# The opening of a two-layer trunk kernel: w_up's first five output tiles fed by feature slices, modulation tile by tile at first, its weights laid out as whole tiles

## The chip, the cores and the metric

The kernel runs on one core of a Trainium2 chip. The metric is the device time of one execution in microseconds, as the median of several runs. A core has a matrix engine (PE), a vector engine (DVE), a scalar engine (ACT), GpSimd (POOL) and a sync engine (SP, which here only issues transfers), and 16 DMA engines that move data between HBM and the on-chip buffer. Each engine has its own list of instructions; semaphores order them against each other. A matmul reads its operands from the on-chip buffer and adds into a PSUM bank.

## The reference, cut to what matters

The whole computation is a two-layer trunk (an mLSTM layer, an attention layer, each followed by a gated feed-forward net) over 256 latent and 256 context tokens of width 1024. The change lies in its first few steps:

```python
def _modulation(cond, w, b):
    m = jax.nn.silu(cond) @ w + b
    return jnp.split(m[:, None, :], 6, axis=-1)

def _modulate(x, shift, scale):
    return x * (1 + scale) + shift
...
        ml = _modulation(c, ada_w[i], ada_b[i])
        mc = _modulation(c_ctx[None, :], ada_w[i], ada_b[i])
        hl = _modulate(x, ml[0], ml[1])
        hc = _modulate(xc, mc[0], mc[1])
...
    x_m = h @ w_up
```

So before the first large product `h @ w_up` (512 tokens x 1024 features by 1024 x 2048) can begin, the shift and the scale of layer 0 (two of the six parts of a 1024 x 6144 product with the two condition vectors) must be known, at least for the features that the product reads first.

## The kernel before

Everything is kept transposed: features on the 128 partitions, the 512 tokens along the row. A product in full precision is made of three matmuls (`mm3`): each operand is split into a rounded part "hi" (made by ACT, a CAST) and the rest "lo" (made by DVE, a subtraction that needs the cast), and hi x hi, hi x lo, lo x hi are added. A split of a tile is therefore always an ACT instruction and then a DVE instruction.

**start_up** does the following, for feature tiles k = 0..7 (128 features each) and the first `NUP` = 5 output tiles m of w_up:

- loads, issued by SP in the order of the table LOADS: `a` loads modulation weights (256 features of shift and scale at a time, GROUPS, eight transfers of 256 KB into four buffers of 512 KB), `x` two feature tiles of tokens (256 KB each), `r` one output tile's weights of w_up, all eight feature tiles of it (512 KB);
- compute, in the order of the table STEPS, which fixes the order on PE, DVE and ACT: `S` splits a buffer of modulation weights, `A` multiplies it with the condition vectors (result `adar`), `C` copies the sums, `T` transposes them on PE (`adat`), `O` adds the bias and writes shift and scale of that group (`mod0`), `E` modulates one token tile (half on DVE, half on ACT), `H` splits it (`hT`), `W` splits half of an output tile's weights, `V` with k and m is one `mm3` of feature tile k into output tile m, `D` some dummy matmuls on zeros. 40 `V` steps make 120 matmuls of 128 x 512.

Group 0 (features 0 to 255) must be whole before any `E`, and with it any `V`, can run. After start_up, `w_up` goes through the other eleven output tiles, 24 matmuls each.

**The weight stream.** From then on all weights come through a class Stream: `_load` issues a 512 KB load into a `raw` buffer (three of them at this stage), `_split` makes hi and lo of it in one of `NB` = 3 buffers with the tag `w`, `use` hands them out. Loads and splits run ahead as far as buffers are free: a split needs a free `w` buffer, a load a free `raw` buffer. In start_up the same three `w` buffers hold the split weights of output tiles 0, 1 and 2, and three `raw` buffers their loads.

**What sets the order.** Only the instructions inside start_up's `manual_schedule` block keep the order of STEPS among themselves. All others, the stream's loads and splits among them, are put into each engine's list by a scheduler that reckons with its own times, and they can come to stand between the steps. Once built, each engine's list is fixed. SP's loads take eight semaphores (DMAHW0 to DMAHW7) in turn, and a load waits for the one that used its semaphore before.

Of the kernel before, what the change touches and what calls it, by code (L numbers as in the profile page):

```python
# [7 lines left out]
F32 = mybir.dt.float32  # L8
F32R = mybir.dt.float32r
# [5 lines left out]
D = 1024  # L15
SEQ = 256
CTX = 256
T = SEQ + CTX
DEPTH = 2
GRID_W = 64  # L20
EPS = 1e-6
# [3 lines left out]
H0 = 4  # L25
H1 = 8
# [3 lines left out]
CW = 1024  # L30

NB, NRAW, NU, NS = 3, 3, 31, 15
# [18 lines left out]
STEPS = (  # L51
# [3 lines left out]
    "W41 V53 C3 T3 O3 V43 E6 V44 V54 V34 H6 V60 V61 V62 E7 H7 V70 V71 V72 V63 V73 V74 V64").split()  # L55

# [17 lines left out]
def _plan():  # L74
# [6 lines left out]

    for m in range(16):
        add(("up", m, 0), 1024)
# [52 lines left out]
def _pack(i):  # L136
    ids, _ = _plan()
    ws = np.zeros((len(ids), 128, CW), np.float32)
# [57 lines left out]
    parts = {  # L196
        "cond": np.stack([col(i["c"][0]), col(i["c_ctx"])], -1).reshape(128, 16),
        "ln_g": col(i["ln_g"]), "ln_b": col(i["ln_b"]),
        "mcw": col(i["m_conv_w"][0]), "mcb": col(i["m_conv_b"][0]),
        "fcw0": col(i["ffn_conv_w"][0]), "fcb0": col(i["ffn_conv_b"][0]),  # L200
        "fcw1": col(i["ffn_conv_w"][1]), "fcb1": col(i["ffn_conv_b"][1]),
        "ada_b": col(i["ada_b"][0, :2 * D]),
        "ada_c": col(i["ada_b"]),
# [4 lines left out]
    for k, v in parts.items():  # L208
# [13 lines left out]
    rope = np.stack([np.tile(cc, (1, H1)), np.tile(ss, (1, H1))], 0).astype(np.float32)  # L222

    tok = np.concatenate([i["ctx"][0], i["x"][0]], 0)
    tokT = np.ascontiguousarray(tok.T.reshape(8, 128, T))
    arrays = {
        "ws": ws, "sm": np.ascontiguousarray(sm), "rope": np.ascontiguousarray(rope),
        "tok": np.ascontiguousarray(tok), "tokT": tokT,
        "ada_w": np.ascontiguousarray(i["ada_w"]),
        "adaT": np.ascontiguousarray(i["ada_w"].transpose(0, 2, 1)).reshape(2, 6, 8, 128, D),  # L230
# [7 lines left out]
class Stream:  # L238
# [20 lines left out]
    def ring(self, j):  # L259
        return [x for x in self.bufs if x[0] <= j][-1]  # L260

    def skip(self, n):
        self.nl = self.ns = self.nu = n

# [93 lines left out]
class K:  # L358
# [36 lines left out]
    def smc(self, name):  # L395
        o, n = self.off[name]
        return self.sm[:, o:o + n]

# [24 lines left out]
    def setup(self):  # L423
        nc, p = self.nc, self.pool
        a = self.a
        self.sm = p.tile([128, a["sm"].shape[1]], F32, name="sm")
        nc.sync.dma_start(self.sm, a["sm"])
        b1 = self.smc("ada_b")[:, 8:16]
# [33 lines left out]

    def ada_mm(self, pr, i, parts):

        for x in parts:
            for kk in range(2):
                k = 2 * i + kk
                self.nc.tensor.matmul(pr[0:4], self.condr[:, k, :], x[:, kk * 512:(kk + 1) * 512],
                                      start=k == 0 and x is parts[0], stop=k == 7 and x is parts[1])

    def ada_copy(self, pr):
        r = self.s2("adarow")
        self.nc.scalar.copy(r[0:4], pr[0:4])
        return r
# [93 lines left out]

    def h_split(self, k):
        h = self.u("hT")  # L570
        self.split(h[:, 0, :], h[:, 1, :], self.xT[k])
        self.hT.append(h)

    def start_up(self):

        nc, st = self.nc, self.st
        self.hT = []
        self.xcd = self.dr.tile([16, 128, 512], F32, name="xcd")
        self.xmd = self.dr.tile([16, 128, 512], F32, name="xmd")
        self.t2d = {(n, p, j): self.dr.tile([128, 1024], F32, name="t2d")  # L580
                    for n, a, b in (("v", 2, 4), ("y", 1, 6)) for p in range(a) for j in range(b)}
        self.xA, self.x1, self.xc, self.xcr = {}, {}, [], []
        w, ps, raws = [], [], []
        src = self.a["ada_w"][0]
        self.adaw, self.xT = {}, []
        for op, g in LOADS:
            f0, f1 = GROUPS[g] if op != "r" else (0, 0)
            if op == "a":
                wd = 128 * (f1 - f0)
                nk = 512 // wd  # L590
                self.adaw[g] = []
                for k in range(8):
                    if k % nk == 0:
                        t = self.uf("adaw")
                        self.adaw[g].append(t)
                    ap = bass.AP(tensor=src.tensor, offset=src.offset + k * 128 * 6 * D + f0 * 128,
                                 ap=[[6 * D, 128], [D, 2], [1, wd]])
                    c = k % nk * 2 * wd
                    nc.sync.dma_start(t[:, c:c + 2 * wd].rearrange("p (a b) -> p a b", a=2), ap)
            elif op == "x":  # L600
                for i in range(f0, f1):
                    x = self.s2("xT")
                    nc.sync.dma_start(x, self.a["tokT"][i])
                    self.xT.append(x)
            else:
                n, _ = st.ids["up", g, 0]
                r = self.pool.tile([128, 1024], F32, tag="raw" if g < 3 else "ar", name="raw0",
                                   bufs=NRAW if g < 3 else 2)
                nc.sync.dma_start(r, st.ws[n])
                raws.append(r)  # L610

        w3 = [self.pool.tile([128, 2, CW], F32R, tag="w", name="w", bufs=NB) for _ in range(3)]

        def wsplit(m, i):
            if i == 0:
                if m < 3:
                    h, l = w3[m][:, 0], w3[m][:, 1]
                elif m == 3:
                    h, l = [self.pool.tile([128, CW], F32R, tag="acc", name="w0", bufs=2) for _ in range(2)]
                else:  # L620
                    h, l = [self.pool.tile([128, CW], F32R, tag="u", name="w0", bufs=NU) for _ in range(2)]
                w.append((h, l))
                ps.append(self.ps("up"))
            c = slice(i * 512, (i + 1) * 512)
            self.split(w[m][0][:, c], w[m][1][:, c], raws[m][:, c])

        e = mybir.EngineType
        idle = self.ps("idle")
        rows, parts, made = {}, {}, [0] * NUP
        with self.tc.manual_schedule(engines={e.PE, e.DVE, e.Activation}):  # L630
            for step in STEPS:
                op, n = step[0], [int(x) for x in step[1:]]
                g = n[0]
                if op == "S":
                    parts[g, n[1]] = self.ada_split(self.adaw[g][n[1]])
                elif op == "A":
                    if n[1] == 0:
                        rows[g] = self.ps("adar")
                    self.ada_mm(rows[g], n[1], parts.pop((g, n[1])))
                elif op == "C":  # L640
                    rows[g] = self.ada_copy(rows[g])
                elif op == "T":
                    rows[g] = self.ada_T(g, rows[g])
                elif op == "O":
                    self.ada_cols(g, rows.pop(g))
                elif op == "E":
                    self.mod_tile(g)
                elif op == "H":
                    self.h_split(g)
                elif op == "W":  # L650
                    wsplit(g, n[1])
                elif op == "V":
                    k, m = n
                    c = slice(k * 128, (k + 1) * 128)
# [3 lines left out]
                else:  # L658
                    for _ in range(g):
                        nc.tensor.matmul(idle, self.zero[:, 0:128], self.zero, start=True, stop=True)  # L660
        for m in range(NUP):
            self.up_evac(m, ps[m])
# [1123 lines left out]
def build(tc, off, a, out):  # L1786
    es = ExitStack()
    with es:
# [4 lines left out]
        k.setup()  # L1793
        st.skip(NUP)
        k.start_up()
# [175 lines left out]
```

## Time and profile before

| what | value |
|---|---|
| median of 3 runs | 1377.26 us (1376.98 to 6290.27) |
| the profiled execution's own time | 1378.52 us |
| its span in the profile | 1376.7 us |
| PE, DVE, ACT busy | 98%, 78%, 52% of the span |
| clock granted to PE, mean | 0.997 |

One of the three runs took 6290.27 us; the other two lie within 0.3 us of each other. The span is the stretch from the first to the last instruction. A row of the timeline reads: start in us, length in us, engine, line of the kernel, operation, output <- input, shapes, how many were merged into the row, and in brackets how long the engine was idle before it and what ended the wait. A table by windows gives for each stretch the busy time of each engine, the share of the DMA engines' time that was used, and the GB/s they moved. PE's matmuls overlap, so their lengths add up to more than the time they take; the distance from start to start is what one costs.

### The profile page before, as it was taken

What the parts mean: (1) busy time and instruction counts of PE and PEld (TensorE: products, weight loads), DVE (VectorE), ACT (ScalarE), POOL (GpSimd) and SP (SyncE); (2) the same over time, 40 slices, a digit from 0 to 9 for tenths busy, and PEclk for the clock granted to TensorE, in tenths of its full rate; (3) what the DMA queues carried; (4) which work ended last, traced back from release to release, by engine and by line L of the source; (5) the groups of instructions that cost most, each with busy time, mean ns of one, the idle gap of its engine ahead of it and who ended that gap; (6) DMA issues with size and microseconds to landing.
All of it is one profiled execution on the core that took longest, in us unless ns stands there. A gap on an engine that the chain in (4) does not pass through costs nothing.

```text
span 1376.7 us, 18622 instructions
## 1 busy us (share of the span) xinstructions
PE 1350.6 (98%) x6581; PEld 1122.9 (82%) x6581; DVE 1075.7 (78%) x1748; ACT 720.9 (52%) x1242; POOL 121.1 (9%) x215
## 2 busy tenths in 40 slices
PE   7999999999999999999999999999999999999997
PEld 3788888888788888878898888888878898888886
DVE  7698756677598696878789978767888889788873
ACT  6675444445544555374643343334556667466660
POOL 0122000011011011120001000000001001000100
PEclk9999999999999999999999999999999999999999
DMA  9789848789666374756747877646897436355760
GB/s 332 240 305 322 283 159 245 240 283 301 218 199 202 104 231 133 250 197 219 243 142 241 300 238 229 223 143 209 297 270 236 140 100 211 103 186 188 253 200 31
DMA packets 97900, 297.58 MB, mean 216 GB/s; under 512 B 12136, under 2 KB 24808, under 8 KB 97808
## 3 DMA queue, kind: packets, MB, share of 16 engines
q1 hardware_dynamic: 68672, 218.52, 48.4%
q0 software_dynamic: 17472, 57.57, 13.3%
q10 hardware_dynamic: 11664, 20.32, 4.0%
q8 instruction: 51, 0.84, 0.2%
q14 instruction: 41, 0.34, 0.1%
HBM read 262.90 MB, written 33.46 MB: 215 GB/s over the span
## 4 chain that ended last, share of the span: by engine, by line
PE 88%; DVE 5%; DMA 4%; ACT 2%; issue 1%; SPq 0%; ACTq 0%; DVEq 0%
PE fin L1313 8%; PE fin L387 6%; PE fin L388 6%; PE fin L389 6%; PE tok L387 6%; PE tok L389 6%; PE tok L388 6%; PE y L388 4%; PE y L389 4%; PE y L387 4%; PE qk L387 4%; PE qk L389 4%; PE qk L388 4%; PE up L388 2%; PE up L387 2%; PE up L389 2%
## 5 line engine op out<-in xcount | busy, mean ns | idle before, releaser
L329 DVE TENSOR_TENSOR w<-raw,w 128x1024 fp32r<-128x1024 f32 (+3 forms) x290 | 347.7, 1202 | 149.5 <-ACT w L326 147.3
L326 ACT CAST w<-raw 128x1024 fp32r<-128x1024 f32 (+3 forms) x290 | 300.1, 1037 | 289.7 <-PE fin L389 78.6
L508 DVE SCALAR_TENSOR_TENSOR junk<-ar,bc 128x1024 f32<-128x1024 f32 x128 | 155.7, 1216 | 4.5 <-ACT bc L550 2.2
L388 PE MATMUL fin<-h,w 128*128 128x512 f32 (+1 forms) x376 | 141.2, 376 | 0.0
L389 PE MATMUL fin<-h,w 128*128 128x512 f32 (+1 forms) x376 | 140.9, 376 | 0.0
L387 PE MATMUL fin<-h,w 128*128 128x512 f32 (+1 forms) x376 | 140.8, 376 | 0.1
L1313 PE MATMUL fin<-h,w 128*128 128x256 f32 (+1 forms) x640 | 112.9, 339 | 0.0
L1313 PEld LDWEIGHTS fin<-h,w 128*128 128x128 f32 x640 | 98.1, 189 | 14.7
L387 PE MATMUL qk<-xc,w 128*128 128x512 f32 x256 | 100.7, 393 | 0.0
L389 PE MATMUL qk<-xc,w 128*128 128x512 f32 x256 | 99.9, 390 | 0.0
L388 PE MATMUL qk<-xc,w 128*128 128x512 f32 x256 | 99.9, 390 | 0.0
L388 PEld LDWEIGHTS fin<-h,w 128*128 128x128 f32 x376 | 70.8, 188 | 13.0 <-DVE h L1205 0.2
L387 PEld LDWEIGHTS fin<-h,w 128*128 128x128 f32 x376 | 70.6, 188 | 13.2 <-ACT h L1204 0.3
L389 PEld LDWEIGHTS fin<-h,w 128*128 128x128 f32 x376 | 70.8, 188 | 12.7
L387 PEld LDWEIGHTS qk<-xc,w 128*128 128x128 f32 x256 | 48.1, 188 | 10.0 <-issue 0.4
L389 PEld LDWEIGHTS qk<-xc,w 128*128 128x128 f32 x256 | 48.1, 188 | 10.0
L388 PEld LDWEIGHTS qk<-xc,w 128*128 128x128 f32 x256 | 48.1, 188 | 9.6
L387 PE MATMUL up<-hT,w 128*128 128x512 f32 x128 | 50.3, 393 | 0.2 <-ACT hT L392 0.2
L388 PE MATMUL up<-hT,w 128*128 128x512 f32 x128 | 50.1, 391 | 0.3 <-DVE hT L393 0.3
L389 PE MATMUL up<-hT,w 128*128 128x512 f32 x128 | 49.9, 390 | 0.0
L389 PE MATMUL tok<-w,hT 128*128 128x512 f32 x128 | 49.8, 389 | 0.0
L387 PE MATMUL tok<-w,hT 128*128 128x512 f32 x128 | 49.8, 389 | 0.0
(455 smaller groups left out, 3152.5 us busy)
## 6 DMA issues: line engine op xcount, KB each, us to landing
raw<-in_ws SPq DMA_DIRECT2D x287, 512.0 KB, 4.4
ar<-in_adaT SPq DMA_DIRECT2D x80, 512.0 KB, 4.6
adaw<-in_ada_w SPq DMA_DIRECT2D x32, 256.0 KB, 6.5
t2d<-raw ACTq DMA_DIRECT2D x13, 512.0 KB, 6.5
raw<-t2d SPq DMA_DIRECT2D x13, 512.0 KB, 4.8
raw<-in_ws POOLq DMA_DIRECT2D x13, 512.0 KB, 7.5
zr<-fd ACTq DMA_DIRECT2D x33, 128.0 KB, 4.3
xmd<-xr POOLq DMA_DIRECT2D x16, 256.0 KB, 4.9
```

The costliest lines, as they stand in the source:

```text
L326: k.nc.scalar.copy(h[:, :cols], src)
L329: k.nc.vector.tensor_sub(l[:, :cols], src, h[:, :cols])
L387: mm(out, w[0], x[0], start=start, stop=False, skip_group_check=on)
L388: mm(out, w[0], x[1], start=False, stop=False, skip_group_check=on)
L389: mm(out, w[1], x[0], start=False, stop=stop, skip_group_check=on)
L508: nc.vector.scalar_tensor_tensor(o, w, 1.0, self.bc[j], op0=ALU.mult, op1=ALU.mult, accum_out=col[:, k, j:j + 1])
L1313: nc.tensor.matmul(o, a, b, start=k == 0 and i == 0, stop=k == 7 and i == 1)
```

## The change

- **Loads.** Modulation weights are packed on the host into whole tiles of 128 x 1024 (`ada0`), one contiguous 512 KB transfer each. Groups are now features 0-127, 128-255, then 256 each (GROUPS), so groups 0 and 1 have two tiles each and the other three four each. The weights of the first five output tiles are loaded by feature tile (`w`, 128 x 640, 320 KB), not by output tile. Of the small constants the 32 columns that the opening needs come first, in a transfer of their own (`sm0`); the others (`s`) come in the middle.
- **Buffers.** Feature slice k = 0, 1, 2 of the weights is split into the three `w` buffers, 3 into the buffer pair `acc`, 4 to 7 into pool buffers `u`. The raw slices lie in `raw`, `ar`, `ar1`, `junk` buffers.
- **Steps.** STEPS is a new table. `A` and `B` are now the products with the hi and the lo part of one tile, each placed by itself; `W` splits a whole slice; the dummy matmuls `D` are gone and eight (`WARM`) stand ahead of everything.
- **Stream.** It no longer holds the first five output tiles, and so needs no `skip`.

```diff
-GROUPS = ((0, 2), (2, 4), (4, 6), (6, 8))
-LOADS = [(c[0], int(c[1])) for c in "a0 a1 x0 r0 r1 r2 x1 r3 a2 r4 x2 a3 x3".split()]
+GROUPS = ((0, 1), (1, 2), (2, 4), (4, 6), (6, 8))
+WARM = 8
+LOADS = (
+    "a00 a01 a10 a11 a20 x0 w0 a21 a22 x1 a23 w1 s a30 a31 a32 a33 w2 x2 x3 w3 a40 a41 w4 a42 x4 w5 a43 w6 x5 x6 "
+    "w7 x7").split()
 STEPS = (
-    "S00 A00 S01 S02 S03 S10 A01 A02 A03 S11 C0 D4 T0 O0 S12 A10 A11 A12 S13 E0 E1 A13 D3 W00 H0 V00 H1 C1 W10 T1 O1 "
...
+    "S00 A00 S01 S10 S11 A01 B01 B00 A11 C0 T0 A10 O0 B10 S20 B11 E0 W0 C1 T1 H0 O1 A20 S21 V03 E1 V04 S22 S23 "
+    "V01 V02 B21 A22 H1 A21 W1 B20 A23 B22 B23 V00 S30 S31 V12 A31 C2 S32 V10 T2 O2 S33 V11 A30 E2 A32 B30 B32 W2"
+    " A33 H2 B31 E3 V13 B33 V14 V20 W3 H3 C3 V23 V32 T3 V24 S40 S41 S42 O3 A40 V30 W4 B40 V33 V31 S43 V22 E4 W5 "
+    "B41 A42 V34 A41 A43 V21 H4 B43 B42 E5 V44 W7 H5 V42 V41 C4 T4 O4 V53 E7 H7 E6 V43 V52 V51 V72 V73 V70 H6 V54"
...
-    for m in range(16):
+    for m in range(NUP, 16):
         add(("up", m, 0), 1024)
...
-    def ada_mm(self, pr, i, parts):
...
+    def ada_mm(self, pr, g, i, x, start, stop):
+
+        n = 256 * (GROUPS[g][1] - GROUPS[g][0])
+        nk = 1024 // n
+        for kk in range(nk):
+            self.nc.tensor.matmul(pr[0:4, :n], self.condr[:, i * nk + kk, :], x[:, kk * n:(kk + 1) * n],
+                                  start=start and kk == 0, stop=stop and kk == nk - 1)
...
-                    c = k % nk * 2 * wd
-                    nc.sync.dma_start(t[:, c:c + 2 * wd].rearrange("p (a b) -> p a b", a=2), ap)
...
+        raw, tag = {}, [("raw", NRAW)] * 3 + [("ar", 2)] * 2 + [("ar1", 1), ("junk", 1), ("raw", NRAW)]
+        nw = NUP * 128
+        for step in LOADS:
+            op, n = step[0], [int(x) for x in step[1:]]
             if op == "a":
...
+                t = raw[step] = self.uf("adaw")
+                src = self.a["ada0"][sum(2 * (f1 - f0) for f0, f1 in GROUPS[:n[0]]) + n[1]]
             elif op == "x":
...
+            elif op == "w":
+                t = raw[step] = self.pool.tile([128, CW], F32, tag=tag[n[0]][0], name="raw0", bufs=tag[n[0]][1])
+                t, src = t[:, :nw], self.a["up0"][n[0]]
             else:
...
+                t, src = self.sm, self.a["sm"]
+            nc.sync.dma_start(t, src)
...
         w3 = [self.pool.tile([128, 2, CW], F32R, tag="w", name="w", bufs=NB) for _ in range(3)]
...
+        w = [(t[:, 0], t[:, 1]) for t in w3]
...
+            for _ in range(WARM):
+                nc.tensor.matmul(idle, self.zero[:, 0:128], self.zero, start=True, stop=True)
...
-                    self.mm3(ps[m], (w[m][0][:, c], w[m][1][:, c]), (self.hT[k][:, 0], self.hT[k][:, 1]),
+                    c = slice(m * 128, (m + 1) * 128)
+                    self.mm3(ps[m], (w[k][0][:, c], w[k][1][:, c]), (hT[k][:, 0], hT[k][:, 1]),
                              made[m] == 0, made[m] == 7)
...
-        st.skip(NUP)
         k.start_up()
```

How the built lists stand is shown at two places; names carry buffer numbers, and the brackets name the semaphores that an instruction waits for.

ACT before, the end of start_up: the last casts of modulation weights (`adas`), of the weights of output tile 4 (`w0_394`) and of the token tiles 6 and 7 (`hT`), then the copies out of the first output tile (`up_280`), and among them the stream's first split (`w_632`, line 326).

```order
L392 CAST adas_480<-adaw_180 128x1024 [waits DMAHW3_49,DMAHW2_49]
L392 CAST w0_394<-raw0_165 128x512
L473 COPY adarow_499<-adar_444 4x512 [waits PE_49]
L567 ACTIVATE xT_183<-xT_183,mod0_84 128x256 [waits DMAHW4_49,DVE_49]
L392 CAST hT_523<-xT_183 128x512 [waits DVE_49,Activation_49]
L567 ACTIVATE xT_185<-xT_185,mod0_84 128x256 [waits DMAHW5_49]
L392 CAST hT_537<-xT_185 128x512 [waits DVE_49,Activation_49]
L679 COPY xr_562<-up_280 128x512 [waits PE_49]
L392 CAST x1_564<-up_280 128x256
L326 CAST w_632<-raw_622 128x1024 [waits DMAHW7_49]
```

ACT now, the middle of start_up: the modulation of token tile 2 (`xT_149`), the cast of slice 2 (`w_181`), then the stream's first split (`w_650`, now line 338), then the casts for token tiles 2 and 3 (`hT_380`, `hT_400`), of slice 3 (`w0_182`) and of group 4's modulation weights (`adas_419`).

```order
L404 CAST adas_359<-adaw_145 128x1024 [waits DMAHW1_49]
L581 ACTIVATE xT_149<-xT_149,mod0_85 128x256 [waits DMAHW3_49,DVE_49]
L404 CAST w_181<-raw0_147 128x640 [waits DMAHW2_49]
L338 CAST w_650<-raw_640 128x1024 [waits DMAHW2_49,PE_49]
L404 CAST hT_380<-xT_149 128x512 [waits DVE_49,Activation_49]
L581 ACTIVATE xT_151<-xT_151,mod0_85 128x256 [waits DMAHW4_49]
L404 CAST w0_182<-raw0_153 128x640 [waits DMAHW5_49]
L404 CAST hT_400<-xT_151 128x512 [waits DVE_49,Activation_49]
L487 COPY adarow_403<-adar_339 4x512 [waits PE_49]
L404 CAST adas_419<-adaw_155 128x1024 [waits DMAHW6_49]
```

The stream's first split has moved from behind the last step of start_up to a place between steps W2 and H2. DVE's half of it stands at the same place in DVE's list, and the stream's second and third split stand further on between later steps.

SP before, the end of start_up's loads: the last modulation weights, token tiles 6 and 7, a tile for later modulations (`ar_778`), the stream's first three loads (`raw_622` to `raw_626`).

```order
L599 DMA adaw_180<-in_ada_w 128x2x256 [waits DMAHW3_49]
L603 DMA xT_183<-in_tokT 128x512 [waits DMAHW4_49]
L603 DMA xT_185<-in_tokT 128x512 [waits DMAHW5_49]
L531 DMA ar_778<-in_adaT 128x1024 [waits DMAHW6_49]
L284 DMA raw_622<-in_ws 128x1024 [waits DMAHW7_49,DVE_49]
L284 DMA raw_624<-in_ws 128x1024 [waits DMAHW0_49,DVE_49]
```

SP now, the same place: token tile 4 (`xT_163`), slices 5 and 6, the last modulation weights (`adaw_167`), token tiles 5, 6, 7, slice 7 (`raw0_175`), and then the stream's first loads (`raw_640`, `raw_642`).

```order
L607 DMA xT_163<-in_tokT 128x512 [waits DMAHW2_49]
L607 DMA raw0_165<-in_up0 128x640 [waits DMAHW3_49]
L607 DMA adaw_167<-in_ada0 128x1024 [waits DMAHW4_49]
L607 DMA raw0_169<-in_up0 128x640 [waits DMAHW5_49]
L607 DMA xT_171<-in_tokT 128x512 [waits DMAHW6_49]
L607 DMA xT_173<-in_tokT 128x512 [waits DMAHW7_49]
L607 DMA xT_177<-in_tokT 128x512 [waits DMAHW0_49]
L607 DMA raw0_175<-in_up0 128x640 [waits DMAHW1_49,DVE_49]
L296 DMA raw_640<-in_ws 128x1024 [waits DMAHW2_49,DVE_49]
L296 DMA raw_642<-in_ws 128x1024 [waits DMAHW3_49,DVE_49]
```

The stream's first load stands behind every load of start_up in both lists; `raw_640`, which the moved split reads, waits among others for the transfer of token tile 4 (DMAHW2).

More of the change, by code (lines that the diff above doesn't have):

```diff
@@ L396, in smc @@
         o, n = self.off[name]
-        return self.sm[:, o:o + n]
+        return self.sm0[:, o:o + n] if o < NSM0 else self.sm[:, o - NSM0:o - NSM0 + n]
     def step(self, q):
@@ L461, in ada_split, with ada_copy @@
         return hi, lo
-    def ada_mm(self, pr, i, parts):
[L465 to L471, printed above, removed]
+    def ada_mm(self, pr, g, i, x, start, stop):
[4 more added lines that the diff above has]
+                                  start=start and kk == 0, stop=stop and kk == nk - 1)
+    def ada_copy(self, pr, g):
         r = self.s2("adarow")
-        self.nc.scalar.copy(r[0:4], pr[0:4])
+        n = 256 * (GROUPS[g][1] - GROUPS[g][0])
+        self.nc.scalar.copy(r[0:4, :n], pr[0:4, :n])
         return r
@@ L627, in start_up @@
+        self.xT = [raw["x%d" % k] for k in range(8)]
+        w3 = [self.pool.tile([128, 2, CW], F32R, tag="w", name="w", bufs=NB) for _ in range(3)]
+        w = [(t[:, 0], t[:, 1]) for t in w3]
+        w.append([self.pool.tile([128, CW], F32R, tag="acc", name="w0", bufs=2) for _ in range(2)])
         e = mybir.EngineType
         idle = self.ps("idle")
[L629 removed]
+        rows, parts, hT = {}, {}, {}
+        todo = {g: 4 * (f1 - f0) for g, (f0, f1) in enumerate(GROUPS)}
@@ L648, in start_up @@
                 elif op == "H":
-                    self.h_split(g)
+                    h = hT[g] = self.u("hT")
+                    self.split(h[:, 0, :], h[:, 1, :], self.xT[g])
                 elif op == "W":
-                    wsplit(g, n[1])
-                elif op == "V":
+                    if g >= len(w):
+                        w += [[self.pool.tile([128, CW], F32R, tag="u", name="w0", bufs=NU) for _ in range(2)]
+                              for _ in range(g + 1 - len(w))]
+                    self.split(w[g][0][:, :nw], w[g][1][:, :nw], raw["w%d" % g][:, :nw])
+                else:
                     k, m = n
-                    c = slice(k * 128, (k + 1) * 128)
-                    self.mm3(ps[m], (w[m][0][:, c], w[m][1][:, c]), (self.hT[k][:, 0], self.hT[k][:, 1]),
+                    if m not in ps:
+                        ps[m] = self.ps("up")
+                    c = slice(m * 128, (m + 1) * 128)
+                    self.mm3(ps[m], (w[k][0][:, c], w[k][1][:, c]), (hT[k][:, 0], hT[k][:, 1]),
                              made[m] == 0, made[m] == 7)
                     made[m] += 1
-                else:
-                    for _ in range(g):
-                        nc.tensor.matmul(idle, self.zero[:, 0:128], self.zero, start=True, stop=True)
+        self.hT = [hT[k] for k in range(8)]
+        raw = parts = w = w3 = rows = None
         for m in range(NUP):
```

77 lines of the change are left out of this document (25 added, 52 removed), and 2 rows, old and new, of the table STEPS.

## The prediction

> **What bounds the kernel now.** I read the page first, then the waits by engine, then the opening by windows and by timeline.
>
> ```profile
> PE 1350.6 (98%) x6581; PEld 1122.9 (82%) x6581; DVE 1075.7 (78%) x1748; ACT 720.9 (52%) x1242; POOL 121.1 (9%) x215
> PE   7999999999999999999999999999999999999997
> ...
> PE adar L468 <- ACT adas L392: 7.0, 1, 7.0
> PE y L388 <- DVE w L329: 2.9, 3, 1.1
> ```
>
> PE is busy in every slice but the first and the last, and its longest wait, 7.0 us, is the first one; the next is 2.9 us in three pieces, far away from the change. So PE's work sets the time, and what start_up does to the moment at which PE has its 120 `up` matmuls behind it should go one to one into the end. PE's timeline in start_up (a row's distance to the next is its cost):
>
> ```profile
> 7.02 1.01 PE L468 MATMUL adar<-adas,condr 128*4 128x512 f32 x2 [7.02 <-ACT adas L392]
> 8.28 5.85 PE L468 MATMUL adar<-adas,condr 128*4 128x512 f32 x14 [0.24 <-DVE adas L393]
> 13.97 1.09 PE L660 MATMUL idle<-zero 128*128 128x512 f32 x4
> ...
> 20.79 0.49 PE L387 MATMUL up<-hT,w 128*128 128x512 f32 x1 [0.16 <-ACT hT L392]
> ...
> 30.92 3.86 PE L468 MATMUL adar<-adas,condr 128*4 128x512 f32 x16
> 34.62 0.39 PE L387 MATMUL up<-hT,w 128*128 128x512 f32 x1
> ...
> 35.45 0.41 PE L480 MATMUL adat<-ident,adarow 4*128 4x4 f32 x4
> 35.79 0.50 PE L387 MATMUL up<-hT,w 128*128 128x512 f32 x1
> ...
> 58.06 0.39 PE L389 MATMUL up<-hT,w 128*128 128x512 f32 x1
> ...
> 59.42 0.39 PE L389 MATMUL up<-hT,w 128*128 128x512 f32 x1
> ```
>
> The first `up` matmul starts at 20.79. From there PE is hardly idle. A group by form over the first 60 us counts the threes:
>
> ```profile
> L389 PE MATMUL up<-hT,w 128*128 128x512 f32 x42 | 16.4, 391 | 0.0
> ```
>
> The 42nd L389 is the one at 59.42; two threes earlier, at 58.06, starts the 120th `up` matmul. That is the mark to compare. Prices: an `up` matmul (59.42 - 58.06) / 6 = 0.227 us, an `adar` matmul (34.62 - 30.92) / 16 = 0.23, a set of four transposes 35.79 - 35.45 = 0.34.
>
> The other side of the opening is the transfers (last two columns: share of the DMA engines' time, GB/s):
>
> ```profile
> 0.00:5.00 5.00, 0.00 (x0) 0.00 (x0) 1.34 (x9) 1.71 (x3) 0.43 (x5) 1.00 0.58 172
> 5.00:10.00 5.00, 2.73 (x7) 0.57 (x8) 2.45 (x2) 2.53 (x3) 0.00 (x0) 1.00 0.96 308
> 10.00:15.00 5.00, 4.93 (x15) 1.55 (x13) 3.68 (x3) 3.68 (x5) 0.00 (x0) 1.00 1.07 344
> 15.00:20.00 5.00, 4.46 (x22) 1.90 (x22) 4.56 (x7) 4.03 (x7) 0.00 (x0) 1.00 1.06 392
> 20.00:25.00 5.00, 4.53 (x21) 2.99 (x20) 4.15 (x10) 4.50 (x10) 0.00 (x0) 1.00 1.04 388
> 25.00:30.00 5.00, 5.00 (x23) 4.12 (x22) 4.97 (x7) 4.55 (x7) 0.00 (x0) 1.00 1.10 353
> 30.00:35.00 5.00, 5.00 (x23) 2.44 (x22) 4.07 (x5) 2.71 (x5) 0.00 (x0) 1.00 1.06 370
> 35.00:40.00 5.00, 5.00 (x25) 3.44 (x24) 3.25 (x7) 3.63 (x7) 0.00 (x0) 1.00 1.09 361
> 40.00:45.00 5.00, 4.99 (x22) 2.94 (x22) 4.29 (x6) 3.94 (x5) 0.00 (x0) 1.00 1.02 406
> ```
>
> The DMA engines are full from 5 to 45 us: 13.44 MB by 40.0. The slowest full windows (308, 344) are those in which only modulation weights come, in pieces of 1 KB; the fastest, 406, has 512 KB tiles with rows of 4 KB.
>
> **The change part by part.** *The earlier start.* Group 0 is half as large, its tiles are contiguous, and the constants ahead of them are small, so the first `up` matmul can start some 7 us earlier: the transfers queued up to slice 0 are 3.2 MB (five modulation tiles, token tile 0, slice 0) instead of 5.5 MB (eight modulation buffers' worth, two token tiles, the constants, one output tile's weights), and 2.3 MB at some 0.33 MB a us are 7 us. PE's total work is the same: the first 16 `adar` matmuls of 512 columns become 32 of 256, the transposes the same, and the seven dummies that go and the eight that come stand where PE waits anyway. All of that would count only if PE then went on without a break.
>
> *The wait that is added.* In the new list of ACT the stream's first split (`w_650`) stands between W2 and H2. It waits for the load `raw_640`, and SP issues that behind every load of start_up. ACT comes to it when slice 2 is cast: sm0, twelve modulation tiles, the other constants, token tiles 0 and 1 and slices 0 to 2 are 8.0 MB, which before's rates move by 25 us; so at about 26.5. Ahead of `raw_640`, with it, stand 16 x 0.524 (modulation) + 8 x 0.262 (tokens) + 8 x 0.328 (slices) + 0.016 + 0.216 (constants) + 0.524 (itself) = 13.86 MB. When is that there? Transfers begin to flow at 2.2 us (0.86 MB by 5.0 at 308 GB/s). The lag from bytes moved to use comes from the first cast of before:
>
> ```profile
> 5.92 1.04 ACT L392 CAST adas<-adaw 128x1024 fp32r<-128x1024 f32 x1 [2.06 <-DMA adaw<-in_ada_w]
> ...
> sm<-in_sm SPq DMA_DIRECT2D x1, 227.0 KB
> ```
>
> It needed 0.76 MB, moved at about 4.65, and ran at 5.92: 1.3 us. At the best window's 406 GB/s the split can start at 2.2 + 13.86 / 0.406 + 1.3 = 37.6; at the rates of before as they are (13.44 MB by 40.0, the rest at 406) at 41.0 + 1.3 = 42.3. Most bytes now come in rows of 4 KB, so I take 39.5, nearer to the fast end. ACT stands from 26.5 to 39.5, and behind it in its list wait H2, E3, W3, H3, C3 and all of group 4; DVE stands at its half of the same split. PE has work up to V14, then V20 needs H2: it stops at about 28.
>
> *What is left at that point.* After the stall come the split, its DVE half and then H2's DVE half, by these rows:
>
> ```profile
> 55.10 1.06 ACT L326 CAST w<-raw 128x1024 fp32r<-128x1024 f32 x1
> ...
> L329 DVE TENSOR_TENSOR w<-raw,w 128x1024 fp32r<-128x1024 f32 x2 | 2.4, 1218 | 0.5 <-ACT w L326 0.5
> L393 DVE TENSOR_TENSOR hT<-xT,hT 128x512 fp32r<-128x512 f32 x8 | 5.3, 687 | 2.5 <-ACT hT L392 2.5
> ```
>
> 39.5 + 1.06 + 1.22 + 0.69 = 42.5 for V20's second matmul. 30 of the 40 `V` steps are still to do: 88 distances to the last one x 0.227 = 20.0; A40 to B43 16 x 0.23 = 3.7; T3 and T4 0.7. One more wait: the stream's third split stands ahead of H4 in ACT's list and takes the buffer of slice 2, so it waits for V21; from there 1.06 + 1.22 + 0.69 = 3.0 to V44's second matmul, of which B43, B42 and V44's first fill 1.1: +1.9. Sum 42.5 + 26.3 = 68.8.
>
> *PE's clock.* PE stands some 13 us. No row of before shows such a break later than the start, but the start shows what follows one: 14 `adar` matmuls in 5.85 us, 0.42 each, against 0.23 later, up to 13.97 where the dummies take 0.27. Nothing lost, if the clock stays up, is one end; the other is 5 us at 0.42 instead of 0.23, 2.3 us. After V20 PE waits for DVE in part, which hides some: I take 1.0. The Trainium skill, "TensorE: Matmul & The Clock Gate", Part 1: The HAM clock gate, says that PE falls to half clock after an idle window of about 3.4 us and comes back after about as long at work; by this the term would be up to 1.6 us, and only the slow start bears on it here.
>
> Last `up` matmul of the 120 at 69.8 against 58.06: +11.7 us. Behind start_up I cost the change at nothing: both lists go on alike, the three first stream tiles are split earlier than before, and PE has 24 matmuls for each of them, 5.4 us, which covers a split of 1.22. If that cover failed, each tile would cost up to what the split is late. The profiled execution would get a span of 1388.4 and a time of 1390.2; it lay 1.3 above the median, so I predict 1377.3 + 11.7 = **1389.0 us**.
>
> **The rivals.** *The load lands early.* SP may issue `raw_640` when token tile 4 is there (11.05 MB: 2.2 + 11.05 / 0.4 + 1.3 = 31.1), and 512 KB tiles can be quick:
>
> ```profile
> raw<-in_ws SPq DMA_DIRECT2D x12, 512.0 KB, 6.4
> ar<-in_adaT SPq DMA_DIRECT2D x3, 512.0 KB, 4.2
> ```
>
> With 4.2 us it is there at 35.3, 4.2 before my 39.5: 1384.8. Against it: with the queue full, the stream's own tiles took 6.4. The Trainium skill, "DMA: Bandwidth & Descriptors", Queues, rings and completion order, says that transfers of one engine need not complete in the order of issue; that would favour this rival. No row shows one overtaking another.
>
> *No stall, and faster.* If the tile were there when ACT reaches the split, V20 would run at about 28 and the last of the 120 at 28.1 + 26.3 = 54.4: 3.7 us less, 1373.6. It breaks even where V20's second matmul starts at 58.06 - 26.3 = 31.8, that is for a landing at 28.8. Against it: 28.8 is before SP can even issue the load.
>
> *Slow transfers and a cold PE.* 42.3 instead of 39.5 and 2.3 instead of 1.0: 1393.1. For it: that is the pace of before.
>
> **How the numbers follow.** Forecast 0.70 (1386 to 1391.5), early landing 0.12, slow and cold 0.13, no stall 0.03; 0.02 for a starved stream or something else that costs more than the stall. Range: early landing to slow and cold, 1384.5 to 1393. 2% is 27.5 us, about what a measurement of this kernel can tell from no change; that would need a landing 16 us later than mine, or a gain larger than the whole wait before 20.79. So faster 0.01, within 2% 0.97, slower 0.02.
>
> **What would show it.** In the profile after: the first `up` matmul near 14 us; a cast `w<-raw` of 128 x 1024 on ACT that starts near 39.5 with about 13 us of idle ahead of it, ended by the transfer; DVE idle as long; PE idle from about 28 to 40.5, then a pause of some 2 us ahead of V44; the 120th `up` matmul near 70, and from there before's distances. I am wrong if that cast waits for less than 5 us, or if the 12 us are gone by the end of w_up.

## The result and the profile after

| | median | runs | profiled execution | its span |
|---|---|---|---|---|
| before | 1377.18 us | 4 (1376.98 to 1377.26, and the one of 6290.27) | 1378.52 us | 1376.7 us |
| after | 1391.97 us | 4 (1390.50 to 1394.86) | 1394.86 us | 1393.1 us |

The medians lie 14.8 us apart. Taken over the fast runs, which leaves out the one of 6290.27, the changed kernel takes 1.0112 times as long as before, with a 95% interval of 1.0100 to 1.0124. Two of its four runs, 1393.30 and 1394.86, lie above the predicted range, the median inside it. The profile is that of the slowest run.

The page of the profile after, its busy time and its 40 slices:

```profile
PE 1356.9 (97%) x6598; PEld 1126.7 (81%) x6598; DVE 1076.6 (77%) x1748; ACT 720.5 (52%) x1241; POOL 121.1 (9%) x215
...
PE   7799999999999999999999999999999999999997
...
PEclk9799999999999999999999999999999999999999
```

Before had this line of the clock:

```profile
PEclk9999999999999999999999999999999999999999
```

Only the second slice has changed (35 to 70 us), on both lines: PE stands in it, and its clock falls to 0.7. The longest wait of PE in the kernel after (total, times, longest):

```profile
PE up L399 <- ACT hT L404: 12.4, 2, 11.6
```

The 7.0 us wait at the start is gone from the top. In its place stands one of 11.6 us, of an `up` matmul for a split token tile. ACT's timeline after says why it is late:

```profile
24.95 0.71 ACT L404 CAST w<-raw 128x640 fp32r<-128x640 f32 x1
39.53 1.04 ACT L338 CAST w<-raw 128x1024 fp32r<-128x1024 f32 x1 [13.86 <-DMA raw<-in_ws]
40.48 0.61 ACT L404 CAST hT<-xT 128x512 fp32r<-128x512 f32 x1
```

And DVE's timeline after at the same place:

```profile
40.60 1.22 DVE L341 TENSOR_TENSOR w<-raw,w 128x1024 fp32r<-128x1024 f32 x1 [14.01 <-ACT w L338]
```

ACT casts slice 2 of the weights, then stands 13.86 us for a transfer of the weight stream, and the H2 that PE needs (40.48) comes behind it. PE's timeline after, a row's distance to the next being its cost:

```profile
14.37 0.50 PE L399 MATMUL up<-hT,w 128*128 128x512 f32 x1
...
29.12 0.39 PE L401 MATMUL up<-hT,w 128*128 128x512 f32 x1
41.14 0.79 PE L399 MATMUL up<-hT,w 128*128 128x512 f32 x1 [11.64 <-ACT hT L404]
42.48 0.79 PE L400 MATMUL up<-hT,w 128*128 128x512 f32 x1 [0.55 <-DVE hT L405]
43.08 0.63 PE L401 MATMUL up<-hT,w 128*128 128x512 f32 x1
43.50 0.63 PE L399 MATMUL up<-hT,w 128*128 128x512 f32 x1
...
48.84 0.39 PE L399 MATMUL up<-hT,w 128*128 128x512 f32 x1
...
57.13 0.51 PE L399 MATMUL up<-hT,w 128*128 128x512 f32 x1 [0.73 <-ACT hT L404]
58.47 0.50 PE L400 MATMUL up<-hT,w 128*128 128x512 f32 x1 [0.84 <-DVE hT L405]
...
61.29 0.63 PE L401 MATMUL up<-hT,w 128*128 128x512 f32 x1
...
62.70 0.39 PE L400 MATMUL up<-hT,w 128*128 128x512 f32 x1
...
73.80 0.39 PE L399 MATMUL up<-hT,w 128*128 128x512 f32 x1
...
133.87 0.39 PE L399 MATMUL tok<-w,hT 128*128 128x512 f32 x1
```

Five things stand in it. The first `up` matmul runs at 14.37 instead of 20.79. PE stops behind the one at 29.12 and goes on at 41.14. From there an `up` matmul takes 0.43 us (43.08 to 43.50) and not 0.23, up to about 48. There is a second pause at 57 to 58, after which matmuls are slow once more, till about 62. And the 120th `up` matmul, counted through the timeline, starts at 73.80 where before had it at 58.06, and the first `tok` matmul, behind w_up, at 133.87:

```profile
118.12 0.39 PE L387 MATMUL tok<-w,hT 128*128 128x512 f32 x1
```

That row is before's. Both marks are 15.7 us late, so nearly all of the 16.4 us that the span has grown is lost before the end of start_up. The windows of the kernel after, with the granted clock and, at the end, the share of the DMA engines and GB/s:

```profile
5.00:10.00 5.00, 3.50 (x15) 1.39 (x15) 3.64 (x3) 4.12 (x4) 0.00 (x0) 1.00 1.02 414
...
30.00:35.00 5.00, 0.00 (x0) 0.00 (x0) 0.00 (x0) 0.00 (x0) 0.00 (x0) 0.66 1.04 397
35.00:40.00 5.00, 0.00 (x0) 0.00 (x0) 0.00 (x0) 0.47 (x1) 0.00 (x0) 0.50 0.79 308
40.00:45.00 5.00, 3.31 (x7) 2.32 (x8) 3.66 (x6) 4.37 (x8) 0.00 (x0) 0.50 0.34 110
45.00:50.00 5.00, 5.00 (x17) 2.98 (x17) 4.96 (x7) 4.44 (x6) 0.00 (x0) 0.64 0.57 190
...
55.00:60.00 5.00, 3.43 (x12) 1.77 (x11) 3.41 (x5) 3.95 (x8) 0.00 (x0) 0.89 0.89 255
60.00:65.00 5.00, 5.00 (x21) 3.69 (x20) 1.76 (x6) 3.55 (x5) 0.00 (x0) 0.77 0.75 263
```

For nearly ten microseconds nothing computes at all, while the DMA engines are full at first (1.04) and busy to 0.79 in the second window. The slow matmuls stand where the granted clock is low.

### The profile page after: what moved, and what is told of

It is laid out like the page before. It is cut to its first block, busy times and chain, and to the rows that moved or that the text cites. A ratio compares the mean times of both kernels' runs of the same rounds, so it can differ in the third digit from the quotient of the medians.

```text
span 1393.1 us, 18632 instructions
## 1 busy us (share of the span) xinstructions
PE 1356.9 (97%) x6598; PEld 1126.7 (81%) x6598; DVE 1076.6 (77%) x1748; ACT 720.5 (52%) x1241; POOL 121.1 (9%) x215
## 4 chain that ended last, share of the span: by engine, by line
PE 87%; DMA 5%; DVE 4%; ACT 2%; issue 1%; ACTq 0%; SPq 0%; DVEq 0%
PE fin L1310 8%; PE fin L399 6%; PE fin L400 6%; PE fin L401 6%; PE tok L399 6%; PE tok L401 6%; PE tok L400 6%; PE y L400 5%; PE y L401 5%; PE y L399 4%; PE qk L399 4%; PE qk L401 4%; PE qk L400 4%; PE up L400 2%; PE up L401 2%; PE up L399 2%
## 5 line engine op out<-in xcount | busy, mean ns | idle before, releaser
L399 PE MATMUL up<-hT,w 128*128 128x512 f32 x128 | 51.9, 407 | 12.4 <-ACT hT L404 12.4
L400 PE MATMUL up<-hT,w 128*128 128x512 f32 x128 | 51.5, 403 | 1.6 <-DVE hT L405 1.6
L401 PE MATMUL up<-hT,w 128*128 128x512 f32 x128 | 51.3, 402 | 0.0
```

The lines of the kernel that those rows point to most:

```text
L399: mm(out, w[0], x[0], start=start, stop=False, skip_group_check=on)
L400: mm(out, w[0], x[1], start=False, stop=False, skip_group_check=on)
L401: mm(out, w[1], x[0], start=False, stop=stop, skip_group_check=on)
```

## The experiments

The theory: the stream's first split stands in ACT's list between W2 and H2 and holds everything behind it until a transfer lands that is queued last; the third does the same, more shortly, ahead of H4; and PE's clock falls in the break. The rival: the opening itself is slow, by the new order of its steps, the slices or the buffers, and the wait only shows where it is late. Before was run on the same chip beside each kernel, 21 times in each of two groups: 1377.11 us beside the first four, 1377.24 beside the last four. The two groups ran on different chips, so a comparison of a kernel of one with a kernel of the other rests on these two medians being alike.

**e1: all three splits behind start_up.** What `issue_after` encloses is put behind the given instruction in that engine's list; `last_act` and `last_dve` are those of start_up's last split. Nothing else in the kernel is changed. The small gate copies for later modulations, which in the changed kernel stand in ACT's list next to the third split, come to stand behind the splits too (the first at 49.45 us in e1, at 53.70 in the first profile).

```diff
-        self.nc.scalar.copy(hi, src)
-        self.nc.vector.tensor_sub(lo, src, hi)
+        a = self.nc.scalar.copy(hi, src)
+        v = self.nc.vector.tensor_sub(lo, src, hi)
+        self.sp = a.ins, v.ins
...
+        self.last_act, self.last_dve = self.sp
...
-            w = st.use(("up", m, 0))
+            if m == NUP:
+                with self.tc.issue_after(self.last_act), self.tc.issue_after(self.last_dve):
+                    w = st.use(("up", m, 0))
+            else:
+                w = st.use(("up", m, 0))
```

> The changed kernel with one thing altered: the stream's first three splits are issued behind the last step of start_up on ACT and on DVE. Loads, buffers, steps and their order stay. Theory (the split that stands in ACT's and DVE's lists between W2 and H2 and waits for a load queued behind all others is the whole loss): no idle stretch of ACT over 3 us between 25 and 50 us, PE not idle ahead of V20, last of the 120 up matmuls near 53 to 54 (V14 ends at 29, then 90 up matmuls x 0.227, 16 adar x 0.23, two sets of transposes 0.34 = 24.8), so 1372 to 1374, 3 to 5 us faster than before. Rival (by the new steps V20 would wait for its own transfers and splits anyway, and the early split only fills that time): PE still idle 8 us or more ahead of V20, 1385 or more.

Measured: 1373.89 us (11 runs, 1372.65 to 1375.80), 0.9980 of before [0.9971, 0.9989]. PE's timeline of e1 at the place of the break, the last matmul of V14 and the first of V20:

```profile
28.70 0.39 PE L401 MATMUL up<-hT,w 128*128 128x512 f32 x1
28.93 0.39 PE L399 MATMUL up<-hT,w 128*128 128x512 f32 x1
...
54.01 0.39 PE L401 MATMUL up<-hT,w 128*128 128x512 f32 x1
```

And ACT's timeline of e1, where the three splits now are:

```profile
46.60 2.95 ACT L338 CAST w<-raw 128x1024 fp32r<-128x1024 f32 x3
```

No break, and the 120th `up` matmul (54.01) is 4.05 us ahead of before's. The same steps, slices, buffers and loads are faster than before once three casts and three subtractions, and with them the small copies, stand elsewhere: the rival falls. The whole loss, 18 us in median, hangs on the place of these instructions in the lists.

**e2: four more transfers ahead of the stream.** They load 4 x 256 KB that nothing reads.

```diff
+        for k in range(4):
+            nc.sync.dma_start(self.s2("more"), self.a["tokT"][k])
```

> The changed kernel with four more transfers of 256 KB, which nothing reads, queued behind token tile 7, ahead of the stream's first load; the order on ACT, DVE and PE stays. Theory (the stall ends when the stream's first tile lands): 1.05 MB at 400 GB/s are 2.6 us, so the first stream split starts near 42.1 instead of 39.5 and the time is 2 to 3.5 us above the changed kernel's, near 1394.5. Rival (the stall ends by something else, a buffer or a token tile): split at 39.5, time as the changed kernel's.

Measured: 1395.73 us (4 runs), 1.0138 of before [1.0124, 1.0151], 3.7 more than the changed kernel beside it (e3). ACT's timeline of e2:

```profile
42.10 1.04 ACT L338 CAST w<-raw 128x1024 fp32r<-128x1024 f32 x1 [16.49 <-DMA raw<-in_ws]
```

1.05 MB ahead of the load put the split 2.6 us later than 39.53 (and e3's 39.48), which is 1.05 MB at 400 GB/s: the landing follows the bytes that are queued ahead. It does not follow the moment of issue: SP issued the load 3.5 us later (35.93 against 32.45), and it landed 2.6 later. The median moved a little more than expected. In this profile the clock falls after the second pause as well, as in the first profile of the change and not as in e3's, and the first `tok` matmul (136.4 against 133.9 there) is 2.5 us later.

**e3: the changed kernel again**, with no edit, to have it on the same chip.

> The changed kernel once more, beside the others on the same chip. Theory and rival alike: 1390 to 1395, the first stream split on ACT near 39.5; what differs from run to run should lie in the matmuls that run at the lower granted clock behind PE's idle stretches.

Measured: 1392.04 us (4 runs, 1391.79 to 1392.52), 1.0109 [1.0095, 1.0123]. Its profiled execution took 1392.13 us, 2.7 less than the first one. PE's timeline and the windows of e3:

```profile
30.00:35.00 5.00, 0.00 (x0) 0.00 (x0) 0.00 (x0) 0.00 (x0) 0.00 (x0) 0.90 1.04 397
...
56.67 0.50 PE L399 MATMUL up<-hT,w 128*128 128x512 f32 x1 [0.73 <-ACT hT L404]
...
60.76 0.40 PE L400 MATMUL up<-hT,w 128*128 128x512 f32 x1
...
71.88 0.39 PE L399 MATMUL up<-hT,w 128*128 128x512 f32 x1
...
55.00:60.00 5.00, 3.43 (x14) 1.78 (x11) 3.58 (x5) 4.40 (x8) 0.00 (x0) 1.00 0.82 265
60.00:65.00 5.00, 5.00 (x25) 4.15 (x25) 2.45 (x7) 4.26 (x7) 0.00 (x0) 1.00 0.68 228
```

The same pause, but the clock stays at 1.00 behind it. From the first matmul of V44 to the one at 60.76 it takes 4.1 us; the first profile needs 5.6 for these (57.13 to 62.70). So 1.5 of the 1.9 us between the 120th `up` matmuls of the two profiles (73.80 and 71.88) is the clock's second fall, which comes in some executions and not in others.

**e4: before, with whole tiles of modulation weights.** One part of the change by itself.

```diff
...
+                for j in range(4):
+                    t = self.uf("adaw")
+                    self.adaw[g].append(t)
+                    nc.sync.dma_start(t, self.a["ada0"][4 * g + j])
...
```

> The kernel before with one part of the change alone: its modulation weights packed as whole 512 KB tiles, one contiguous transfer each instead of two of 256 KB in pieces of 1 KB; groups, steps and everything else as before. Theory (the opening of the kernel before is paced by these transfers, 308 to 344 GB/s against 400): the first up matmul 2 to 3.5 us earlier (20.8 to about 18), 1373.5 to 1375.5. Rival (it is paced by ACT's and DVE's splits, or by the PE work behind): less than 1 us gained.

Measured: 1375.60 us (11 runs), 0.9987 [0.9978, 0.9996]: 1.5 us less than before. The windows and PE's timeline of e4:

```profile
5.00:10.00 5.00, 2.90 (x6) 0.27 (x6) 2.11 (x2) 2.77 (x3) 0.00 (x0) 1.00 0.99 366
```

```profile
6.10 1.01 PE L474 MATMUL adar<-adas,condr 128*4 128x512 f32 x2 [6.10 <-ACT adas L398]
...
19.56 0.50 PE L393 MATMUL up<-hT,w 128*128 128x512 f32 x1
```

The transfers are quicker (366 GB/s against 308 in this window, 411 against 344 in the next), but the first `up` matmul comes only 1.2 us earlier, not the 2 to 3.5 that were expected. The likely reason, not shown by a run, is that all of group 0 must still be split and multiplied first. The layout is worth about half of e1's gain; the smaller first group and the slices, which are what is left of the change, were not tested apart.

**e5: the third split alone behind start_up**, and with it the two small gate copies of the same place. The first stays between W2 and H2 and the second behind S40 (39.67 and 44.93 us on ACT).

```diff
-            self._split()
+            if self.ns == 2:
+                with self.k.tc.issue_after(self.k.last_act), self.k.tc.issue_after(self.k.last_dve):
+                    self._split()
+            else:
+                self._split()
...
-            self.tick(0, ADA_U)
+            with self.tc.issue_after(self.last_act), self.tc.issue_after(self.last_dve):
+                self.tick(0, ADA_U)
```

> The changed kernel with the stream's third split and the copies for later modulations (gate) issued behind the last step of start_up; its first and second split stay where they are in ACT's and DVE's lists. Theory (the pause ahead of V44 is the third split's wait for V21, and the second stretch at the lower clock follows from that pause): first split again near 39.5, no pause ahead of V44, 2 to 4.5 us less than the changed kernel, 1388 to 1390. Rival (that pause would be there anyway, by H4's own inputs): as the changed kernel, 1391.5 to 1393.

Measured: 1389.18 us (4 runs), 1.0089 [1.0075, 1.0103], 2.9 less than e3. No pause ahead of V44 and no second fall of the clock. PE's timeline of e5 after the break:

```profile
42.63 0.79 PE L404 MATMUL up<-hT,w 128*128 128x512 f32 x1 [0.55 <-DVE hT L409]
...
47.76 0.39 PE L403 MATMUL up<-hT,w 128*128 128x512 f32 x1
```

The first break is as before, and the 120th `up` matmul is at 69.10. So the third split with the copies costs 2 to 3 us, and the first two the rest of the 18. Of the two that were moved here the split's wait ends last: in the first profile the copies ran at 53.70 us and the split, which waits for V21, at 55.51.

**e6: e5, with PE kept at work in the break** by 48 matmuls on zeros, whose sums nothing reads: STEPS has `D48` between V14 and V20.

```diff
+                elif op == "D":
+                    for _ in range(g):
+                        nc.tensor.matmul(idle, self.zero[:, 0:128], self.zero, start=True, stop=True)
```

> The kernel of e5_third_split_behind with 48 dummy matmuls on zeros on PE between V14 and V20, in PE's idle stretch (48 x 0.227 = 10.9 us of the 12); every other list stays as it is. Theory (behind the stall some 13 up matmuls run at half clock, 0.43 us each instead of 0.227): granted clock 1.00 from 40 us on, distances of 0.23 behind V20, 2 to 3 us less than e5_third_split_behind, 1385.5 to 1387.5. Rival (after the stall ACT and DVE pace PE, the clock costs nothing): same time as e5_third_split_behind.

Measured: 1387.68 us (5 runs), 1.0078 [1.0064, 1.0092], against e5's 1389.18. PE's timeline of e6 and one of its windows:

```profile
29.27 11.05 PE L655 MATMUL idle<-zero 128*128 128x512 f32 x48
41.32 0.49 PE L403 MATMUL up<-hT,w 128*128 128x512 f32 x1 [1.00 <-ACT hT L408]
42.66 0.50 PE L404 MATMUL up<-hT,w 128*128 128x512 f32 x1 [0.85 <-DVE hT L409]
...
43.93 0.39 PE L403 MATMUL up<-hT,w 128*128 128x512 f32 x1
44.42 0.50 PE L404 MATMUL up<-hT,w 128*128 128x512 f32 x1
...
46.70 0.40 PE L403 MATMUL up<-hT,w 128*128 128x512 f32 x1
...
40.00:45.00 5.00, 3.04 (x11) 1.53 (x9) 3.58 (x5) 4.37 (x8) 0.00 (x0) 1.00 0.34 108
```

The clock is at 1.00, and V20's second matmul is where it was in e5. From it to the matmul behind the A40 pair takes 4.04 us (42.66 to 46.70), against 5.13 in e5 and 6.36 in the first profile of the change. So the clock is a cost, but of 1.1 us in this pair of profiles and 1.5 in the medians, where 2 to 3 were expected (the intervals against before overlap, the runs themselves do not): with the clock up PE waits for DVE instead (43.93 to 44.42, one distance of 0.49).

**e7: the same order of steps, other buffers.** The three `w` buffers go to the slices that are read last (5, 6, 7), the pool buffers to slices 0, 1, 2. A split of the stream then has no free buffer until the end of start_up.

```diff
-        w = [(t[:, 0], t[:, 1]) for t in w3]
-        w.append([self.pool.tile([128, CW], F32R, tag="acc", name="w0", bufs=2) for _ in range(2)])
+        w = {5 + j: (t[:, 0], t[:, 1]) for j, t in enumerate(w3)}
+        w[3] = [self.pool.tile([128, CW], F32R, tag="acc", name="w0", bufs=2) for _ in range(2)]
```

> The changed kernel with the three w buffers given to slices 5, 6 and 7 instead of 0, 1 and 2, and pool buffers to 0, 1, 2; nothing is said of the order. Theory (the scheduler puts the stream's splits into the middle of start_up because there the buffers of slices 0 to 2 come free): the splits stand behind start_up's steps again, no idle stretch of PE ahead of V20, 1372.5 to 1375, as e1_splits_behind. Rival (the splits go forward for another cause, or the pool runs short): 1385 or more.

Measured: 1374.46 us (11 runs), 0.9980 [0.9971, 0.9988]. ACT's timeline of e7:

```profile
49.54 1.05 ACT L338 CAST w<-raw 128x1024 fp32r<-128x1024 f32 x1 [2.29 <-PE up L401]
```

The split has moved to the end of start_up by itself. It waits for PE there, and PE for nothing. So what let the scheduler put it early was that a buffer came free early; with e1 this makes two independent ways to the same time.

**e8: e1 without the eight dummy matmuls** that the change puts at the start (`WARM = 0`).

> The kernel of e1_splits_behind without the eight dummy matmuls at the start. Theory (until the first up matmul ACT, DVE and the transfers pace PE): first up matmul within 0.5 us of 13.9, time within 1 us of e1_splits_behind, 1373 to 1375. Rival (the dummies are what brings the clock up in time): adar matmuls of 256 columns at 0.21 instead of 0.11 up to about 13 us, first up matmul 1.5 us later or more, 1375.5 or more.

Measured: 1374.10 us (11 runs), 0.9978 [0.9969, 0.9987], 0.2 from e1 and not told apart from it. PE's timeline of e8, then that of e1:

```profile
8.68 2.67 PE L482 MATMUL adar<-adas,condr 128*4 128x256 f32 x12 [0.24 <-DVE adas L405]
...
14.24 0.50 PE L399 MATMUL up<-hT,w 128*128 128x512 f32 x1
```

```profile
8.61 2.06 PE L482 MATMUL adar<-adas,condr 128*4 128x256 f32 x12 [0.25 <-DVE adas L405]
...
13.91 0.50 PE L399 MATMUL up<-hT,w 128*128 128x512 f32 x1
```

In this pair the kernel with the dummies does twelve products in 0.6 us less and has its first `up` matmul 0.33 earlier. That is no more than kernels with the dummies differ among themselves: the same twelve products took 2.58 us in the first profile of the change, and the first `up` matmul of the others stands between 13.91 (e1) and 14.64 (e7). No effect of the dummies is shown.

e1, e7 and e8 beat both kernels, by 3 us against before.

## Why the prediction was right, and where a size was off

The direction, the place and the mechanism were right, and e1 and e7 show the mechanism from two sides. The time, 1391.97, is 3.0 above the 1389.0 that was forecast: the mark of the 120th `up` matmul stands at 73.80 and not at 69.8. Step by step:

- **The earlier start.** "some 7 us earlier" was 6.4 (14.37 against 20.79). Right.
- **The wait that is added.** ACT at the split: 25.7 instead of 26.5 (39.53 less 13.86). The landing: 39.53 against 39.5. e2 shows that the reason given was right, the bytes queued ahead; that it came to within 0.03 is luck, since 39.5 was a choice between 37.6 and 42.3. DVE stands 14.01 us at its half, and PE stops at 29.3 instead of 28.
- **What is left.** V20's second matmul: 42.48 against 42.5. The pause ahead of V44 was put at 1.9 us. Without it V44's second matmul would follow four `adar` and one `up` matmul behind 55.31, at about 56.5; it came at 58.47. That is 2.0, and right.
- **PE's clock: this is the term of the sum that was mis-sized.** The prediction says "After V20 PE waits for DVE in part, which hides some: I take 1.0", with 2.3 as the upper end. Against e6, whose clock stays up, the first profile loses 6.36 - 4.04 = 2.3 us after the break, and 5.57 - 4.09 = 1.5 against e3 after the second pause, which the prediction did not price at all: 3.8 in place of 1.0. In e3 only the first is there, 5.94 - 4.04 = 1.9 (42.44 to 48.38). The reason why little would be hidden stands in e6: only about 0.3 us of waiting for DVE appears when the clock is up. The row from which the prediction took its 0.42, the 14 `adar` matmuls from 8.28, lies in windows where the trace of before has the granted clock at 1.00, so it did not show a lowered clock; that the matmuls behind the break, at a clock of 0.50, take the same 0.43 was not to be read from it.
- **How long the slow matmuls go on.** The Trainium skill, "TensorE: Matmul & The Clock Gate", Part 1: The HAM clock gate, says that the window in which activity is counted, some 3.4 us, is free-running. As an estimate from this section of the Trainium skill, the slow stretch may then last nearly two windows, since the clock returns only at the end of a busy one; the 1.6 us that the prediction worked out by it is one window. The traces agree that the length varies: from V20's second matmul on, those at 0.43 us go on for about 3.2 us in e5 (to 45.8) and 5.9 in the first profile (to 48.4).
- **The small pieces.** 20.0 + 3.7 + 0.7 = 24.4 us were worked out from V20's second matmul on, pause and clock aside. e6, which has neither, takes 25.4 (42.66 to 68.04). One us was missing: the wait for DVE at 43.93 (0.26 us), and some 0.1 us at each of six places, most of them beside another kind of matmul, where the distance is 0.33 and not 0.23.
- **Behind start_up** the change was costed at nothing. The first `tok` matmul is 15.75 us late, just as the mark at the 120th (15.74). The span is 16.4 longer; the 0.7 between is no more than what other profiles differ by there (e1 gains 4.05 at the mark and 5.5 in the span).

For the first profile the sum then closes. Its mark is 4.0 late against the forecast: 2.8 by the clock, 1.0 by the small pieces, 0.1 by the pause. That execution is the slowest of four, one with both falls of the clock. In e3 the mark is 2.1 late (71.88): 0.9 by the clock, 1.0 by the small pieces. Its profiled execution, 1392.13, lies 1.9 above the 1390.2 that was forecast for a profiled one. The rest of the 3.0 between the medians is the 1.3 us that the forecast took off because before's profiled execution lay that much above its median; e3's lies 0.1 above.

The rivals. *The load lands early*: no. SP's timeline after has the issue of the load and of the two behind it:

```profile
32.45 9.73 SPq L296 DMA_DIRECT2D raw<-in_ws  x3
```

From issue (32.45) to use (39.53) it took 7.1 us with the queue full, not 4.2. The remark of the Trainium skill, "DMA: Bandwidth & Descriptors", Queues, rings and completion order, that transfers need not complete in their order of issue did not help this rival here: the 2.6 us of e2 fit a landing in order. *Slow transfers and a cold PE*: half of it came, the cold PE, and past the end of its price, while the transfers were as fast as forecast; that is why the median lies between it and the forecast. *No stall, and faster*: not in this kernel, but e1 comes near to the kernel it describes. It gave 54.4 for the mark and 1373.6 for the time without the stall; e1 has 54.01 and 1373.89. That the mark is so near is luck in part: V20's second matmul stands at 29.16 and not at 28.1, and the pause of 1.9 us that is in the 54.4 is not in e1. So the gain that the change was worth, 3.2 us, was there, and 18 us of wait were laid over it.

How much of this is what can be read from the mark of the 120th in the profiles: e1 54.01, e6 68.04, e5 69.10, e3 71.88, the first one 73.80, which is 19.8 in all between the first and the last. The break itself costs 14.0, the clock behind it 1.1, the third split 2.8 with the clock that differs between e5 and e3, the second fall and a longer first one 1.9.

What decides in an execution whether the clock falls at the second pause is not shown by an experiment. The two profiles of one kernel differ in it with the same recorded waits (0.73 and 0.84 us). The last section gives a rule that fits both, read from the profiles afterwards.

## What to carry to other kernels

When a change frees a buffer earlier, look for what is waiting for such a buffer: a prefetching instruction may move forward in an in-order list, ahead of work that is ready, and hold it until a transfer lands that is queued behind everything. Compare the place of the instruction in its engine's list with the place of its transfer in the queue; to mend it, pin the instruction behind the stage (e1), or give the buffers that it needs to what is freed last (e7). And price a break on PE at more than its length: some microseconds at half clock follow (1.1 to 2.3 us of loss here), and a short pause soon after can bring them again.

## What the runs showed of the hardware that was not expected

- In these profiles the granted clock changes only at ticks 3.41 us apart. Read in stretches of a quarter of a microsecond, it falls at 31.58, returns at 48.64, falls at 58.88 and returns at 62.30 in the first profile, distances of 17.06, 10.24 and 3.42 us, or 5, 3 and 1 ticks. e2 has the same three distances (33.90, 50.96, 61.20, 64.61), e3 has 13.66, or 4 (34.01 and 47.67), and e5 4 as well (32.21 and 45.87). The ticks lie differently in each execution. So the time from PE's last matmul to the fall varies: 2.1 us in the first profile, 4.7 in e3.
- What counts seems to be how long PE was busy between two ticks. In the first 140 us of the five profiles in which the clock falls (the first one, e2, e3, e5, e6) it fell after each tick interval with 1.84 us of PE busy or less and stayed up after each with 1.96 or more. It returned after intervals with 2.88 us or more, and not after one with 2.87. Across the second pause the interval has 1.84 us in the first profile (55.47 to 58.88) and 1.96 in e3 (54.49 to 57.90): the same pause, cut differently by the ticks. This rule was fitted to the profiles afterwards, and no run tests it.
- So no whole idle interval is needed: a pause with 0.73 and 0.84 us of recorded waiting was enough. By the same section of the Trainium skill, "TensorE: Matmul & The Clock Gate", Part 1, it takes an idle window of about 3.4 us; here the measurement goes against it.
- With rows of 2 to 4 KB, most of them 4, the DMA engines moved 397 to 414 GB/s in every full window of the kernel after, from 5 to 35 us; with pieces of 1 KB before had 308 and 344.
